# A two-layer diffusion block: buffers and queue order of the first layer's modulation, and the shape of three later modulation units

## The chip, the cores and the metric

The kernel runs on one core of one Trainium2 chip. The metric is the device time of one execution in microseconds (us); lower is better. One more execution was recorded by the hardware profiler; its own time stands beside the others below.

## The reference, cut to what matters

Two layers work on 512 latent tokens and 256 context tokens of width 1024. At the head of each layer a vector `c` (for the latents) and a vector `c_ctx` (for the context) give six modulation vectors through one matrix product each; the first two of them shift and scale the normalised tokens before the input projection.

```python
mod = (c_act @ w_mod[l] + b_mod[l])[:, None, :]
sh1, sc1, g1, sh2, sc2, g2 = jnp.split(mod, 6, axis=-1)
modc = cc_act @ w_mod[l] + b_mod[l]          # the same for the context
h  = rms_norm(x,  g_mix[l]) * (1 + sc1)  + sh1
hc = rms_norm(xc, g_mix[l]) * (1 + csc1) + csh1
aq, ak, av, bu, bv, cin, dq, dk, dv = split_cols(h @ w_in[l])
# four head groups (attention, gating, pooling, attention), then
x = x + g1 * (mix @ w_out[l])
x = x + g2 * swiglu(rms_norm(x, g_ffn[l]) * (1 + sc2) + sh2, ...)
```

## The kernel before

Data is feature-major: 8 tiles `x[k]` of 128 features by 768 tokens. Weights are split into a high and a low part (`wsplit`, L75: ScalarE copies at L82, VectorE subtracts at L83), and a product of two split operands is three matmuls (`mm3`, L63, lines L65 to L67). The kernel is written as a program without an order between engines; a planner with a simulated clock makes the order of each engine's queue from it when the kernel is built, and each queue then runs strictly in that order. `issue_after(x)` tells the planner that what stands in its block comes behind `x` in the queue of `x`'s engine. Tiles of one tag share a fixed number of buffers (`BUFS`), PSUM banks likewise (`BANKS`).

**The start of layer 0.** The string `START` (L27) gives the order in which steps are written down: `s` is a modulation slab (`mod_slab`, L193), `x` a load of a token tile with its squares, `w` the load and split of half of the first three weight units. Slab k holds the shift and the scale for feature tile k: it is 1 MB of weights, loaded as two halves of 512 KB into the tag `h` (8 buffers). Its 8 matmuls (L200) have 32 output partitions and 256 columns each, four of them side by side in PSUM bank `md`; ScalarE copies the result into a tile `rows` of tag `mraw` (L203), TensorE transposes it into bank `tq` (L143), and three small VectorE operations (L206 to L208) make shift and scale. Then `scaled` (L248, at L253 and L254) makes `hu[k]`, the scaled and split token tile. Slabs 4 to 7 take the `h` buffers that slabs 0 to 3 leave.

The norm runs beside it. `norm_scale` (L287) sums the squares on TensorE (L292, bank `tq`) and takes the inverse root on VectorE; `norm_spread` (L296) spreads it over the partitions (L302) and ScalarE evicts it (L304). They are written behind slab 4 and slab 5, and both spreads use bank `md`, so in that bank they stand ahead of slabs 6 and 7.

Then for k = 0 to 7 the three first units multiply `hu[k]` (`scaled_proj`, L260, from L441: a round of 18 matmuls), and a fourth unit, `win_dv` 1, does the same over all k in banks `tq` and `md` with its weights in tag `mraw` (L443 to L445). `normalise` (L448) makes the normalised tiles `h[k]` on VectorE, ScalarE and GpSimd (L312 to L317), for k from 2 on behind `hu[7]` in the queues. `d_proj(0)` is the first to multiply them (`tok_proj`, L550), from bank `pj`, which `c_take` (L795, at L799) has to empty first.

**Later units.** `mod_unit` (L146) is called three times in layer 0 (L893, L898, L902) for the units 4, 2 and 3. For each of four pairs of 512 KB pieces in tag `mraw` (2 buffers) it issues four matmuls of 32 output partitions and 512 columns, two for each piece (L154); rows are copied (L157), transposed in four steps and added up by four VectorE operations (L138). The planner fits these matmuls between those of the head groups.

Of the kernel before, what the change touches and what calls it, by code (L numbers as in the profile page):

```python
# [11 lines left out]
AF = mybir.ActivationFunctionType  # L12
OP = mybir.AluOpType
# [4 lines left out]
KT = 8  # L18
# [6 lines left out]
ORDER = (4, 6, 5, 7, 0, 2, 3, 1)  # L25

START = "s0 x1 x0 s1 w0 x2 x3 s2 x4 x5 s3 x6 x7 w1 s4 s5 s6 s7"  # L27
EPS = 1e-6
BIG = 1e30
W = 24 + NT  # L30
# [9 lines left out]
def hybrid_block(ctx: ExitStack, tc, t, out):  # L40
    nc = tc.nc
    V, S, G, T = nc.vector, nc.scalar, nc.gpsimd, nc.tensor
# [7 lines left out]
    def tile(tag, shape, dtype=F32):  # L50
        return sb.tile(shape, dtype, tag=tag, name=tag, bufs=BUFS[tag])

    def psum(tag):
        return psp.tile([128, 512], F32, tag=tag, name=tag, bufs=BANKS[tag])
# [14 lines left out]
    def load_raw(src, tag, size=1024):  # L69
        n = src.free_size()  # L70
        raw = tile(tag, [128, size])
        nc.sync.dma_start(raw[:, :n], src)
        return raw[:, :n]
# [43 lines left out]
        return x  # L117

    cc = const_tile("cc", [128, KT, 2], t["cc"])
    slabs = {k: [load_raw(t["wslab"][k, i], "h") for i in range(2)] for k in range(1)}  # L120
    ident = const_tile("ident", [128, 128], t["ident"])
    ones = const_tile("ones", [128, 32])
    V.memset(ones, 1.0)
    cact = const_tile("cact", [128, KT, 32])
# [7 lines left out]
    def mod_out(mods, pt, groups):  # L132

        m, bm = mods["m"], mods["bm"]
        for u, n, v, cols in groups:
            for i, c in enumerate(cols):
                b = bm[:, u, n].unsqueeze(2).to_broadcast([128, 4, v]) if i == 0 else m[:, u, n, :, 0:v]
                V.tensor_tensor(m[:, u, n, :, 0:v], pt[:, :, c], b, op=OP.add)  # L138

    def transposed(rows, n, tag="md"):  # L140
        pt = psum(tag).rearrange("p (s q) -> p s q", q=128)
        for s in range(n):
            T.transpose(pt[:, s, :], rows[:, 128 * s:128 * s + 128], ident)  # L143
        return pt

    def mod_unit(u, mods, tag="mraw"):  # L146

        ps = psum("md")
        for kk in range(4):
            raws = [load_raw(t["wmod"][mods["l"], u, 2 * kk + i], tag) for i in range(2)]  # L150
            for i in range(2):
                for n in range(2):
                    j = 2 * i + n
                    T.matmul(ps[32 * j:32 * j + 32, :], cact[:, 2 * kk + i, :],  # L154
                             raws[i][:, 512 * n:512 * n + 512], start=kk == 0, stop=kk == 3)
        rows = tile("mraw", [128, 512])
        S.activation(rows, ps, AF.Copy)  # L157
        pt = transposed(rows, 4)
        mod_out(mods, pt, [(u, n, 2, (slice(32 * n, 32 * n + 2), slice(64 + 32 * n, 66 + 32 * n))) for n in range(2)])

    def mod_vector(units, mods, v):

# [30 lines left out]
    def mod_slab(k, mods, bg):  # L193

        m, bm, l = mods["m"], mods["bm"], mods["l"]
        ps = psum("md")
        for i in range(2):
            raw = slabs[k][i] if k in slabs else load_raw(t["wslab"][k, i], "h")
            for j in range(4):
                T.matmul(ps[32 * j:32 * j + 32, :256], cact[:, 4 * i + j, :], raw[:, 256 * j:256 * j + 256],  # L200
                         start=i == 0, stop=i == 1)
        rows = tile("mraw", [128, 512])
        S.activation(rows[:, :256], ps[:, :256], AF.Copy)  # L203
        pt = transposed(rows, 2, "tq")
        red = small.tile([128, 2, 2], F32, tag="red", name="red")
        V.tensor_reduce(red, pt[:, 0:2].rearrange("p s (j x) -> p s x j", x=32)[:, :, 0:2], axis=AX.X, op=OP.add)  # L206
        V.tensor_scalar(m[:, k // 4, 0, k % 4], red[:, 0], bm[:, k // 4, 0, k % 4:k % 4 + 1], None, op0=OP.add)
        V.tensor_scalar(mods["a"][:, 0, k], red[:, 1], mods["g"][:, 0, k:k + 1], bg[:, k:k + 1],  # L208
                        op0=OP.mult, op1=OP.add)

    def new_mod(l):
        return {"l": l, "m": const.tile([128, 6, 2, 4, 2], F32, name=f"mod{l}"),
# [17 lines left out]
    segs_all = ((0, SEQ, 0), (SEQ, NT, 1))  # L230
# [29 lines left out]
    def scaled_proj(w, h, cuts, pss, k):  # L260
        for (c0, c1, *_), ps in zip(cuts[0], pss):
            mm3(ps[:, :c1 - c0], wf(w, k, 0), wf(w, k, 1), h[:, 0, c0:c1], h[:, 1, c0:c1], k == 0, k == KT - 1)
# [22 lines left out]
    marks = {}  # L285

    def norm_scale(sq, segs):  # L287

        n = segs[-1][1] // 128
        ps = psum("tq")  # L290
        for i in range(n):
            marks["scale"] = T.matmul(ps[:, i:i + 1], sq.acc[:, 128 * i:128 * i + 128], ones[:, 0:1],  # L292
                                      start=True, stop=True)
        return rsqrt(ps[:, :n], n, 1.0 / D, EPS)

# [78 lines left out]
    mods = [new_mod(0)]  # L374
# [11 lines left out]
    for l in range(DEPTH):  # L386
# [13 lines left out]
        if l == 0:  # L400
            xs, hu, ready = [None] * KT, [None] * KT, set()
            sq = Squares(segs_all)
            ws = [[], [], []]
            for what, k in START.split():
                k = int(k)
                if what == "w":
                    for w, (name, g) in zip(ws, first):
                        w += wsplit(t[name][0, g][:, 512 * k:512 * k + 512])
                    continue
                if what == "s":  # L410
                    mod_slab(k, mods[0], bg)
                else:
                    xs[k] = load_x(t["xt"][:, k])
                    sq.add(xs[k], G if k in (1, 3, 4, 5, 6, 7) else V)
                if k in ready:
                    hu[k] = scaled(xs[k], a[:, 0, k], shift(k), segs_all)
                ready.add(k)
                if what + str(k) == "s4":
                    rr = norm_scale(sq, segs_all)
                if what + str(k) == "s5":  # L420
                    r = norm_spread(rr, segs_all, ("md", "md"))
            first = ws
            mods.append(new_mod(1))
        else:
            r = norm_spread(norm_scale(sq, segs_all), segs_all, ("tq", "md"))
            first = [feat_units(*x) for x in first]
        fcuts = [cuts_lat if last else cuts_all] * 2 + [cuts_all]
        pss = [[psum(x) for x in y] for y in (("pj", "pj"), ("sc", "sc"), ("po", "pt"))]
        if last:

            for j, (w, ct, ps) in enumerate(zip(first, fcuts, pss)):
                for k in range(KT):
                    with ExitStack() as st:
                        for mark, n in (("scale", 6), ("spread", 10)):
                            if 8 * j + k >= n:
                                st.enter_context(tc.issue_after(marks[mark].ins))
                        scaled_proj(w, hu[k], ct, ps, k)
        else:
            for k in range(KT):
                for w, ct, ps in zip(first, fcuts, pss):  # L440
                    scaled_proj(w, hu[k], ct, ps, k)  # L441
        pss.append([psum(x) for x in ("tq", "md")])
        w = feat_units("win_dv", 1, "mraw")  # L443
        for k in range(KT):
# [485 lines left out]
        h = []  # L930
# [184 lines left out]
```

## Time and profile before

| | us |
|---|---|
| median of three runs | 1545.6 |
| lowest and highest | 1543.95, 1546.96 |
| the profiled execution | 1543.86 |
| its span, first to last instruction | 1542.1 |
| TensorE busy in the span | 1508.3 |
| VectorE busy | 956.9 |
| ScalarE busy | 618.8 |

The span is what the profiler's records cover; the execution's own time is 1.8 us longer. Where a time of an instruction is named below, it counts from the start of the span. Engines: PE is TensorE, PEld its weight loads, DVE VectorE, ACT ScalarE, POOL GpSimd, SP the engine whose queue issues the loads.

### The profile page before, as it was taken

What the parts mean: (1) busy time and instruction counts of PE and PEld (TensorE: products, weight loads), DVE (VectorE), ACT (ScalarE), POOL (GpSimd) and SP (SyncE); (2) the same over time, 40 slices, a digit from 0 to 9 for tenths busy, and PEclk for the clock granted to TensorE, in tenths of its full rate; (3) what the DMA queues carried; (4) which work ended last, traced back from release to release, by engine and by line L of the source; (5) the groups of instructions that cost most, each with busy time, mean ns of one, the idle gap of its engine ahead of it and who ended that gap; (6) DMA issues with size and microseconds to landing.
All of it is one profiled execution on the core that took longest, in us unless ns stands there. A gap on an engine that the chain in (4) does not pass through costs nothing.

```text
span 1542.1 us, 26166 instructions
## 1 busy us (share of the span) xinstructions
PE 1508.3 (98%) x10098; PEld 1330.2 (86%) x10098; DVE 956.9 (62%) x2317; ACT 618.8 (40%) x1278; POOL 118.3 (8%) x107
## 2 busy tenths in 40 slices
PE   6899999999999999999999999899999999999999
PEld 4788787788888888888888888889889998998997
DVE  3789877686485624843375458899865443544453
ACT  5547655643322112221222344477654332332331
POOL 2521200100000000000000004542000000000000
PEclk9999999999999999999999999999999999999999
DMA  8443223342243313722273232201232233233223
GB/s 313 128 144 102 93 80 108 126 141 76 89 144 111 122 62 101 234 62 63 82 230 96 71 105 76 83 32 44 89 101 90 93 94 98 90 88 105 89 86 100
DMA packets 79324, 163.39 MB, mean 106 GB/s; under 512 B 12000, under 2 KB 17760, under 8 KB 79200
## 3 DMA queue, kind: packets, MB, share of 16 engines
q1 hardware_dynamic: 79200, 161.73, 32.8%
q8 instruction: 79, 1.29, 0.3%
q14 instruction: 45, 0.37, 0.1%
HBM read 157.50 MB, written 4.19 MB: 105 GB/s over the span
## 4 chain that ended last, share of the span: by engine, by line
PE 87%; DVE 6%; DMA 4%; ACT 2%; issue 1%; POOL 1%; SPq 0%; ACTq 0%; POOLq 0%
PE pj L65 9%; PE pj L66 9%; PE pj L67 9%; PE sc L66 6%; PE sc L65 6%; PE sc L67 6%; PE tq L65 3%; PE tq L66 3%; PE tq L67 3%; PE po L66 3%; PE po L65 3%; PE po L67 3%; PE po L350 2%; PE pt L66 2%; PE pt L65 2%; PE pt L67 2%
## 5 line engine op out<-in xcount | busy, mean ns | idle before, releaser
L82 ACT ACTIVATE w<-raw 128x512 fp32r<-128x512 f32 x368 | 227.1, 621 | 617.6 <-PE sc L67 154.2
L83 DVE TENSOR_TENSOR w<-raw,w 128x512 fp32r<-128x512 f32 x336 | 226.7, 677 | 242.9 <-ACT w L82 242.6
L65 PE MATMUL pj<-w,h 128*128 128x256 f32 x480 | 138.4, 289 | 6.7 <-DVE post L499 5.9
L66 PE MATMUL pj<-w,h 128*128 128x256 f32 x480 | 138.7, 289 | 0.0
L67 PE MATMUL pj<-w,h 128*128 128x256 f32 x480 | 137.7, 287 | 0.0
L65 PE MATMUL pj<-st,w 128*128 128x258 f32 (+2 forms) x384 | 120.4, 314 | 2.5 <-ACT st L253 2.3
L66 PE MATMUL pj<-st,w 128*128 128x258 f32 (+2 forms) x384 | 120.0, 313 | 0.0
L66 PE MATMUL sc<-st,w 128*128 128x258 f32 (+2 forms) x384 | 119.8, 312 | 0.0
L65 PE MATMUL sc<-st,w 128*128 128x258 f32 (+2 forms) x384 | 119.7, 312 | 0.0
L67 PE MATMUL pj<-st,w 128*128 128x258 f32 (+2 forms) x384 | 119.5, 312 | 0.0
L67 PE MATMUL sc<-st,w 128*128 128x258 f32 (+2 forms) x384 | 118.9, 310 | 0.0
L65 PEld LDWEIGHTS pj<-w,h 128*128 128x128 f32 x480 | 92.1, 192 | 13.9 <-ACT post L494 5.5
L83 POOL TENSOR_TENSOR w<-raw,w 128x512 fp32r<-128x512 f32 x32 | 43.0, 1354 | 739.0 <-DVE row L283 633.3
L66 PEld LDWEIGHTS pj<-w,h 128*128 128x128 f32 x480 | 92.4, 192 | 1.7 <-DVE post L499 0.8
L67 PEld LDWEIGHTS pj<-w,h 128*128 128x128 f32 x480 | 92.3, 192 | 0.3 <-issue 0.2
L65 PEld LDWEIGHTS pj<-st,w 128*128 128x128 f32 x384 | 73.1, 190 | 9.5 <-ACT st L253 3.5
L67 PEld LDWEIGHTS pj<-st,w 128*128 128x128 f32 x384 | 72.6, 189 | 5.5 <-issue 1.7
L65 PEld LDWEIGHTS sc<-st,w 128*128 128x128 f32 x384 | 73.2, 191 | 4.5
L66 PEld LDWEIGHTS pj<-st,w 128*128 128x128 f32 x384 | 72.7, 189 | 4.8 <-issue 0.4
L66 PEld LDWEIGHTS sc<-st,w 128*128 128x128 f32 x384 | 72.7, 189 | 4.2
L67 PEld LDWEIGHTS sc<-st,w 128*128 128x128 f32 x384 | 72.3, 189 | 4.0
L65 PE MATMUL po<-st,w 128*128 128x512 f32 (+1 forms) x192 | 66.2, 345 | 0.0
(308 smaller groups left out, 4117.9 us busy)
## 6 DMA issues: line engine op xcount, KB each, us to landing
mraw<-in_wmod SPq DMA_DIRECT2D x80, 512.0 KB, 3.9
raw<-in_wg SPq DMA_DIRECT2D x88, 256.0 KB, 2.5
raw<-in_wu SPq DMA_DIRECT2D x88, 256.0 KB, 2.6
raw<-in_wd SPq DMA_DIRECT2D x64, 256.0 KB, 2.7
h<-in_wslab SPq DMA_DIRECT2D x16, 512.0 KB, 8.1
raw<-in_wout SPq DMA_DIRECT2D x32, 256.0 KB, 2.6
x<-in_xt SPq DMA_DIRECT2D x16, 384.0 KB, 5.4
raw<-in_wd SPq DMA_DIRECT2D x32, 192.0 KB, 2.4
```

The lines of the kernel that those rows point to most:

```text
L65: T.matmul(ps, ah, bh, start=start, stop=False)
L66: T.matmul(ps, ah, bl, start=False, stop=False)
L67: T.matmul(ps, al, bh, start=False, stop=stop)
L82: S.activation(w[:, 0, :n], raw, AF.Copy)
L83: eng.tensor_sub(w[:, 1, :n], raw, w[:, 0, :n].bitcast(F32))
L350: T.matmul(o[64 * hh:64 * hh + 64, :128], vs[hh][lo:hi], pts[i, hh], start=i == 0, stop=i == n - 1)
```

## The change

Slabs 1 to 3 stay in tag `h`, slab 4 is loaded into the two buffers of `mraw`, and slabs 5, 6 and 7 are loaded as four pieces of 256 KB each into buffers of `pts`, `T`, `post` and `bias`, tags that the head groups use later. So no slab has to wait for the buffer of another one. `rows` moves from `mraw` (two buffers) to `br` (one buffer, used next by the load of `d_k_gain`). `norm_scale` and `norm_spread` are written behind slab 7; the spread for the context uses bank `tq`, the one for the latents `md`. The rounds of products for k = 3, 4 and 5 are put behind the last transpose of slab 5, 6 and 7 in TensorE's queue (k = 6 and 7 behind that of slab 7 too), the round for k = 7 also behind the last matmul of the spread. `mod_unit` takes one 512 KB piece at a time and makes four matmuls of 256 columns from it, side by side in four groups of partitions, over eight pieces; it then needs a copy of 256 columns, two transposes and one VectorE operation.

```diff
+SPARE = {5: ("pts", "pts", "pts", "T"), 6: ("post", "post", "post", "post"), 7: ("T", "T", "bias", "bias")}
     def mod_unit(u, mods, tag="mraw"):
         ps = psum("md")
-        for kk in range(4):
-            raws = [load_raw(t["wmod"][mods["l"], u, 2 * kk + i], tag) for i in range(2)]
-            for i in range(2):
-                for n in range(2):
-                    j = 2 * i + n
-                    T.matmul(ps[32 * j:32 * j + 32, :], cact[:, 2 * kk + i, :],
-                             raws[i][:, 512 * n:512 * n + 512], start=kk == 0, stop=kk == 3)
+        for k in range(KT):
+            raw = load_raw(t["wmod"][mods["l"], u, k], tag)
+            for j in range(4):
+                T.matmul(ps[32 * j:32 * j + 32, :256], cact[:, k, :], raw[:, 256 * j:256 * j + 256],
+                         start=k == 0, stop=k == KT - 1)
         rows = tile("mraw", [128, 512])
-        S.activation(rows, ps, AF.Copy)
-        pt = transposed(rows, 4)
-        mod_out(mods, pt, [(u, n, 2, (slice(32 * n, 32 * n + 2), slice(64 + 32 * n, 66 + 32 * n))) for n in range(2)])
+        S.activation(rows[:, :256], ps[:, :256], AF.Copy)
+        pt = transposed(rows, 2)
+        V.tensor_tensor(m[:, u].rearrange("p n (j s) v -> p (n j) s v", s=2), ...)
     def mod_slab(k, mods, bg):
-            raw = slabs[k][i] if k in slabs else load_raw(t["wslab"][k, i], "h")
+            raws = slabs[k][2 * i:2 * i + 2] if k in SPARE else [slabs[k][i][:, x:x + 512] for x in (0, 512)]
-        rows = tile("mraw", [128, 512])
+        rows = tile("br", [128, 256])
+    def slab_load(k):
+        if k in SPARE:
+            slabs[k] = [load_raw(t["wslab"][k, x // 2][:, 512 * (x % 2):512 * (x % 2) + 512], tag, 512)
+                        for x, tag in enumerate(SPARE[k])]
+        elif k:
+            slabs[k] = [load_raw(t["wslab"][k, i], "mraw" if k == 4 else "h") for i in range(2)]
                 if what == "s":
+                    slab_load(k)
                     mod_slab(k, mods[0], bg)
-                if what + str(k) == "s4":
-                    rr = norm_scale(sq, segs_all)
-                if what + str(k) == "s5":
-                    r = norm_spread(rr, segs_all, ("md", "md"))
+            rr = norm_scale(sq, segs_all)
+            r = norm_spread(rr, segs_all, ("md", "tq"))
             for k in range(KT):
-                for w, ct, ps in zip(first, fcuts, pss):
-                    scaled_proj(w, hu[k], ct, ps, k)
+                with ExitStack() as st:
+                    if k > 2:
+                        st.enter_context(tc.issue_after(slab_end[min(k + 2, KT - 1)].ins))
+                    if k > 6:
+                        st.enter_context(tc.issue_after(marks["spread"].ins))
+                    for w, ct, ps in zip(first, fcuts, pss):
+                        scaled_proj(w, hu[k], ct, ps, k)
```

## Rows read from the trace of the kernel before

**Rows 1.** The page, part 1: busy time, share of span, instructions, by engine.
```profile
PE 1508.3 (98%) x10098; PEld 1330.2 (86%) x10098; DVE 956.9 (62%) x2317; ACT 618.8 (40%) x1278; POOL 118.3 (8%) x107
```
**Rows 2.** Windows: stretch, length, busy us by engine (instructions), PE clock, DMA share, GB/s.
```profile
0.00:72.50 72.50, 55.94 (x360) 40.44 (x360) 41.41 (x97) 38.79 (x78) 29.46 (x25) 0.98 0.65 227
72.50:280.00 207.50, 203.41 (x1606) 169.75 (x1606) 168.44 (x552) 121.95 (x293) 25.93 (x25) 1.00 0.33 108
```
**Rows 3.** Timeline of SP's queue: start, duration, line, what is loaded.
```profile
24.78 0.33 SPq L72 DMA_DIRECT2D raw<-in_win_dv  x1
...
35.93 0.43 SPq L464 DMA_DIRECT2D b_v_gain<-in_b_v_gain  x1
...
42.68 0.64 SPq L72 DMA_DIRECT2D h<-in_wslab  x1
```
**Rows 4.** Time to landing of the loads issued at 24.78 and at 42.68.
```profile
DMA to landing us min/median/max: 8.8/8.8/8.8
...
DMA to landing us min/median/max: 7.2/7.2/7.2
```
**Rows 5.** Windows inside the start, columns as in the second group.
```profile
4.00:32.00 28.00, 20.76 (x134) 12.76 (x134) 11.63 (x28) 14.71 (x29) 9.16 (x5) 1.00 1.02 388
...
47.80:55.60 7.80, 3.47 (x39) 1.56 (x39) 6.14 (x11) 6.34 (x14) 5.51 (x6) 1.00 0.34 124
55.60:58.60 3.00, 3.00 (x9) 2.52 (x10) 3.00 (x8) 2.23 (x6) 0.97 (x1) 0.50 0.64 208
```
**Rows 6.** Timeline of PE: start, duration, line, tiles, shapes, count [idle before, releaser].
```profile
26.38 0.51 PE L65 MATMUL pj<-st,w 128*128 128x512 f32 x1 [0.47 <-ACT st L253]
...
29.98 0.64 PE L200 MATMUL md<-h,cact 128*32 128x256 f32 x8
...
36.78 1.07 PE L200 MATMUL md<-h,cact 128*32 128x256 f32 x16
37.78 1.50 PE L292 MATMUL tq<-ones,row 128*128 128x1 f32 x12
...
49.43 1.07 PE L200 MATMUL md<-h,cact 128*32 128x256 f32 x16 [1.64 <-ACT row L304]
...
72.52 0.39 PE L65 MATMUL pj<-w,h 128*128 128x256 f32 x1 [0.56 <-DVE x L799]
```
**Rows 7.** Timeline of ACT: the second eviction of the spread norm.
```profile
48.80 0.57 ACT L304 ACTIVATE row<-md 128x512 f32<-128x512 f32 x1
```
**Rows 8.** Groups by line, DVE, 47.8 to 82.6 us: count, busy us, mean ns.
```profile
L317 DVE SCALAR_TENSOR_TENSOR h<-x,mod,h 128x256 fp32r<-128x256 f32 x8 | 6.5, 847 | 2.3 <-ACT h L316 2.3
L317 DVE SCALAR_TENSOR_TENSOR h<-x,mod,h 128x512 fp32r<-128x512 f32 x8 | 6.5, 818 | 0.0
L83 DVE TENSOR_TENSOR w<-raw,w 128x512 fp32r<-128x512 f32 x6 | 4.3, 744 | 0.0
L315 DVE SCALAR_TENSOR_TENSOR x<-x,a,row 128x512 f32<-128x512 f32 x4 | 2.7, 739 | 0.0
L315 DVE SCALAR_TENSOR_TENSOR x<-x,a,row 128x256 f32<-128x256 f32 x4 | 2.1, 558 | 0.0
```
**Rows 9.** Groups by line, PE, 72 to 300 us: the three later units and their transposes.
```profile
L154 PE MATMUL md<-mraw,cact 128*32 128x512 f32 x96 | 23.2, 604 | 2.1 <-DMA mraw<-in_wmod 1.1 <-issue 1.1
L143 PE MATMUL md<-ident,mraw 128*128 128x128 f32 x12 | 1.9, 277 | 0.0
```
**Rows 10.** Timeline of PE: groups of narrow matmuls, and what starts behind two of them.
```profile
20.44 0.64 PE L200 MATMUL md<-h,cact 128*32 128x256 f32 x8
21.01 0.50 PE L66 MATMUL pj<-st,w 128*128 128x512 f32 x1
...
155.65 1.04 PE L154 MATMUL md<-mraw,cact 128*32 128x512 f32 x2
156.62 0.55 PE L350 MATMUL po<-pts,row 128*64 128x128 f32 x6
...
252.86 1.07 PE L154 MATMUL md<-mraw,cact 128*32 128x512 f32 x8
```

More of the change, by code (lines that the diff above doesn't have):

```diff
@@ L119, in hybrid_block @@
     cc = const_tile("cc", [128, KT, 2], t["cc"])
-    slabs = {k: [load_raw(t["wslab"][k, i], "h") for i in range(2)] for k in range(1)}
+    slabs = {0: [load_raw(t["wslab"][0, i], "h") for i in range(2)]}
     ident = const_tile("ident", [128, 128], t["ident"])
@@ L138, in mod_out, with transposed @@
                 V.tensor_tensor(m[:, u, n, :, 0:v], pt[:, :, c], b, op=OP.add)
-    def transposed(rows, n, tag="md"):
+    slab_end = {}
+    def transposed(rows, n, tag="md", k=None):
         pt = psum(tag).rearrange("p (s q) -> p s q", q=128)
         for s in range(n):
-            T.transpose(pt[:, s, :], rows[:, 128 * s:128 * s + 128], ident)
+            slab_end[k] = T.transpose(pt[:, s, :], rows[:, 128 * s:128 * s + 128], ident)
         return pt
     def mod_unit(u, mods, tag="mraw"):
+        m, bm = mods["m"], mods["bm"]
         ps = psum("md")
-        for kk in range(4):
-            raws = [load_raw(t["wmod"][mods["l"], u, 2 * kk + i], tag) for i in range(2)]
-            for i in range(2):
-                for n in range(2):
-                    j = 2 * i + n
-                    T.matmul(ps[32 * j:32 * j + 32, :], cact[:, 2 * kk + i, :],
-                             raws[i][:, 512 * n:512 * n + 512], start=kk == 0, stop=kk == 3)
-        rows = tile("mraw", [128, 512])
-        S.activation(rows, ps, AF.Copy)
-        pt = transposed(rows, 4)
-        mod_out(mods, pt, [(u, n, 2, (slice(32 * n, 32 * n + 2), slice(64 + 32 * n, 66 + 32 * n))) for n in range(2)])
+        for k in range(KT):
[3 more added lines that the diff above has]
+                         start=k == 0, stop=k == KT - 1)
+        rows = tile("mraw", [128, 512])
+        S.activation(rows[:, :256], ps[:, :256], AF.Copy)
+        pt = transposed(rows, 2)
+        V.tensor_tensor(m[:, u].rearrange("p n (j s) v -> p (n j) s v", s=2),
+                        pt[:, 0:2].rearrange("p s (j x) -> p j s x", x=32)[:, :, :, 0:2],
+                        bm[:, u].rearrange("p n (j s) -> p (n j) s", s=2).unsqueeze(3).to_broadcast([128, 4, 2, 2]),
+                        op=OP.add)
     def mod_vector(units, mods, v):
@@ L197, in mod_slab @@
         for i in range(2):
-            raw = slabs[k][i] if k in slabs else load_raw(t["wslab"][k, i], "h")
+            raws = slabs[k][2 * i:2 * i + 2] if k in SPARE else [slabs[k][i][:, x:x + 512] for x in (0, 512)]
             for j in range(4):
-                T.matmul(ps[32 * j:32 * j + 32, :256], cact[:, 4 * i + j, :], raw[:, 256 * j:256 * j + 256],
-                         start=i == 0, stop=i == 1)
-        rows = tile("mraw", [128, 512])
-        S.activation(rows[:, :256], ps[:, :256], AF.Copy)
-        pt = transposed(rows, 2, "tq")
+                T.matmul(ps[32 * j:32 * j + 32, :256], cact[:, 4 * i + j, :],
+                         raws[j // 2][:, 256 * (j % 2):256 * (j % 2) + 256], start=i == 0, stop=i == 1)
+        rows = tile("br", [128, 256])
+        S.activation(rows, ps[:, :256], AF.Copy)
+        pt = transposed(rows, 2, "tq", k)
         red = small.tile([128, 2, 2], F32, tag="red", name="red")
```

## The prediction, made before the changed kernel was run

> **What bounds the kernel now.** I read the page's busy times first: TensorE is busy 1508.3 us, 98% of the span, and VectorE 62% [rows 1]. So what counts is a TensorE stretch that is idle, or work taken off TensorE. The windows by stage say where either can be found [rows 2]: of the first 72.5 us TensorE is busy for 55.9, so 16.6 us are idle there; from 72.5 to 280 us it is busy for 203.4 of 207.5, so there only less TensorE work helps, and VectorE with 168.4 of 207.5 us is not far behind. The change touches these two stretches and nothing later.
>
> Inside the start the reader should see two things. Up to 32 us the loads are the limit: they move 388 GB/s with the DMA engines full [rows 5]. From 47.8 to 55.6 us TensorE works for 3.5 of 7.8 us [rows 5], and neither loads nor arithmetic explain that: slab 6 waits 1.64 us for ScalarE to empty bank `md` of the spread norm [rows 6, 7], and slab 7 stands behind slab 6. Slab 7's last half was issued only at 42.68 us, behind small loads such as the broadcast gain at 35.93, and landed 7.2 us later, at 49.9 [rows 3, 4]. After the idle stretch the granted clock is 0.50 for 3 us, the 1.2 GHz level [rows 5]. The first product of `d_proj` comes at 72.52 us, 0.56 us after its bank was wanted [rows 6].
>
> **Change, part 1: own buffers, and the order in the start.** Slabs 6 and 7 no longer wait for `h` buffers, so their loads can stand right behind slab 5 and the second weights. The last of those weights was issued at 24.78 and landed 8.8 us later, at 33.6 [rows 3, 4]; slab 5 was issued before it. Behind it come 2.1 MB of slabs 6 and 7: at 388 GB/s [rows 5] 5.4 us, so slab 7 lands at about 39 instead of 49.9 us.
>
> TensorE then goes so: the round for k = 3 is held behind slab 5's transposes, at about 34 us (slab 5 there by 33.6, then the second half of its matmuls, a copy, two transposes). From there it has to do, until `d_proj`: five rounds of products of 3.5 us each (26.38 to 29.98 holds one round and a pair of transposes) [rows 6], 17.5; slabs 6 and 7 at 1.0 us each (36.78 to 37.78) [rows 6] and 0.3 for two transposes (12 take 1.9 us) [rows 9], 2.6; the column sums 1.5 [rows 6] and the spread, as many narrow matmuls, taken as the same, 3.0; `win_dv` 1, six matmuls for each k where a round has eighteen, a third of 8 x 3.5, 9.3. The sum is 32.4, so 66.4 us, and with 0.6 us for the gaps at the slabs 67 instead of 72.5: **5.5 us gained**. The half clock after 55.6 us goes with the idle stretch and is in this sum.
>
> What could take its place: `normalise`. The norm stands behind slab 7 now. Slab 7's transposes are done at about 41; before, the second spread was evicted at 49.4, 10 us behind the end of the column sums at 39.3 [rows 6, 7]. With 8 to 10 us again r is there at 49 to 52, no earlier than before. From there VectorE needs 6.5 + 6.5 + 2.7 + 2.1 us for the normalised tiles and 4 x 0.74 for the weight splits of `d_proj(0)` [rows 8], 20.8 us, so it ends at 70 to 73, while TensorE starts the context tiles at 67 and needs the last latent tile later. I take no cost for this; the other end is 3.5 us lost to the latent tiles. That is also why I don't count all of the 16.6 idle us.
>
> New waits, each with its queue. The rounds for k = 3 to 7 stand behind transposes in TensorE's queue, which runs in order: a late slab holds them and everything behind them; that is the second rival. `rows` has one buffer, so ScalarE's copy of the next slab waits for two transposes, 0.3 us [rows 9], beside loads that arrive 2.7 us apart (1 MB at 388 GB/s) [rows 5]: nothing, at most 0.3 us a slab. The load of `d_k_gain` waits in SP's queue for slab 7's transposes, with the `bias` and `win_d` loads behind it, from 35 to 41 us or later; the work that hides it is the rest of the start, 26 us of TensorE; without this cover it would cost its 6 us. The memset for `wpool` and the first `bias` tiles wait for slabs 6 and 7, long before they are needed: nothing.
>
> Between the ends (3.5 us lost to the latent tiles; 3.5 us more if `d_proj` profits from VectorE's earlier work too) part 1 gives 2 to 9 us, and I take 5.5, the value that the rows add up to.
>
> **Piece size, a rule against the change.** Half a slab in one load flowed at 388 GB/s beside 256 KB weight pieces [rows 5], so I price pieces at the same rate. The Trainium skill, page "DMA: Bandwidth & Descriptors", section "Rules for kernel authors", asks for at least 1 MiB in one DMA for the most bandwidth, and its fit gives a fixed 2.0 us with each; an estimate from that, if eight pieces of 256 KB went one behind the other at 2.6 us, puts slab 7's landing at 54 us. The windows speak against it, since many loads are in flight at once.
>
> **Change, part 2: three units in pieces.** A narrow matmul uses 32 of the 128 output partitions, and four of them run side by side if they stand together: one alone holds TensorE for 0.97 us (155.65 to 156.62), and a group of four has a record of 1.07 against its 1.04 [rows 10]. Before, two matmuls come with each piece, and the planner cut most groups in two: 24 pieces make some 22 groups of about a microsecond, 23.2 us in sum [rows 9], 21.7 without the overlap with what follows (1.04 - 0.97 for each). After it, a piece brings four matmuls of 256 columns, which have the form of half a slab: 0.57 us (20.44 to 21.01) [rows 10]. 24 x 0.57 = 13.7 us, so 8.0 us of TensorE go. Half of the twelve transposes go too, 1.9 us in all [rows 9]: at most 0.9, I take 0.5. VectorE and ScalarE lose a little work. **8.5 us of TensorE work** is the upper end. Not all of it need reach the end: TensorE is idle for only 4.1 us here, VectorE is busy for 81% [rows 2], and these matmuls now fill time in which a softmax runs on other engines. With that cover gone some waits show. I bound it at a half, 4 us, and at all, 8.5, and take three quarters, **6.3 us**, since TensorE is the fuller engine by 35 us. Two waits of 1.1 us for pieces [rows 9] can stay or go; they are inside these bounds.
>
> **Sum.** The profiled execution took 1543.86 us, its span 1542.1. 1543.9 - 5.5 - 6.3 = 1532.1. The median is 1.7 us above that execution, so **1533.8 us**. With both parts at their low and high ends: 1528 to 1540.
>
> **Rivals.**
> First, the start gives nothing: r is no earlier and VectorE's 20.8 us of normalising [rows 8] are the new limit. For it: r waits for slab 7 now. Against it: `hu[7]`, behind which most of `normalise` stands, is ready some 10 us earlier. Part 2 alone: 1539.3.
>
> Second, slower: slab 7 lands late and holds the last three rounds and the norm. Its place is TensorE's queue between 41 and 55 us. Each microsecond of landing behind 39 costs one; the 5.5 are used up at 44.5, the 6.3 of part 2 at 51, and from 54 us on the kernel is slower by more than 0.2%. For it: SP's issues run behind one another, and in the kernel before the same slab landed at 49.9 [rows 3, 4]; a stalled TensorE fell to the half clock [rows 5]. Against it: the pieces have buffers of their own, and the 388 GB/s. At 55 us: 1549. By the rule of the Trainium skill above it would be this case.
>
> Third, the change doesn't do what it says: the planner cuts each piece's four matmuls in two, as it cut the groups before. Then 48 x 0.57 = 27.4 us instead of 21.7 [rows 9, 10], 5.7 lost against 5.5 gained: 1545.8. Against it: all four now wait for one load, and slabs ran as whole groups [rows 6].
>
> Fourth, all of it arrives: 9 and 8.5 us, 1528.
>
> **How the numbers follow.** Forecast 0.62, start gives nothing 0.17, late slab 0.07, cut groups 0.07, all of it 0.07. A measurement of this kernel can tell about 0.2%, 3 us, from no change. Forecast, fourth and most of the first are faster by more than that: 0.83. The cut groups and a little of the first are the same: 0.09. Slower: 0.08, the late slab and a planner's order that comes out worse. The range takes in the bounds of both parts, 3 us for the order that the planner makes anew, and the first rival: 1525 to 1543; it leaves out the second and the third.
>
> **What would show it.** Right: slab 7 lands near 39 us; no gap above 2 us and no half clock between 40 and 60; the first `pj<-w,h` product of `d_proj` near 67; the later units 24 groups of 8 records, some 14 us in sum. Wrong: that product as late as before, with VectorE never idle behind r (first rival); TensorE waiting for slab 6 or 7 (second); groups of 4 records or fewer (third); TensorE gaps from 80 to 280 us grown by more than 4 us (the units' gain not passed on).

## The result and the profile after

The changed kernel takes **1556.1 us** (median; 1553.2 to 1557.5) beside 1545.0 us for the kernel before on the same chip, a ratio of **1.0067, 95% interval 1.0052 to 1.0081**: slower by about two thirds of a per cent, where 1533.8 us was forecast and 1543 was the upper end of the range. The profiled execution took 1557.5 us, its span is 1555.7, so there are 13.6 us to explain (1555.7 - 1542.1).

First the page, part 1, and the windows of [rows 2] again (stretch, length, busy us and instructions for PE, PEld, DVE, ACT and POOL, then PE clock, DMA share, GB/s).

```profile
PE 1514.9 (97%) x10188; PEld 1338.5 (86%) x10188; DVE 960.2 (62%) x2308; ACT 619.8 (40%) x1278; POOL 113.9 (7%) x107
```
```profile
0.00:72.50 72.50, 55.36 (x337) 38.92 (x338) 39.68 (x88) 39.02 (x79) 22.30 (x23) 0.91 0.64 227
72.50:280.00 207.50, 197.98 (x1615) 170.82 (x1613) 165.61 (x518) 115.31 (x273) 26.43 (x26) 0.97 0.30 96
```

TensorE was to be busy for less and is busy for 6.6 us more. The clock says why: 0.91 and 0.97 in the two stretches that had 0.98 and 1.00 [rows 2]. Where that time lies is seen in narrower windows of TensorE alone (stretch, length, busy, clock, DMA share, GB/s):

```profile
30.00:35.50 5.50, 3.33 (x20) 0.74 1.05 391
35.50:39.50 4.00, 4.00 (x14) 0.51 0.67 209
...
60.00:65.00 5.00, 4.17 (x16) 0.50 0.16 42
65.00:70.00 5.00, 5.00 (x26) 0.83 0.03 11
...
80.00:85.00 5.00, 3.13 (x15) 0.54 0.48 157
85.00:90.00 5.00, 5.00 (x35) 0.78 0.00 0
125.00:140.00 15.00, 12.39 (x82) 0.77 0.64 209
```

Four times the clock falls to 0.50, the 1.2 GHz level (the longer windows hold stretches at both levels). Busy time multiplied by the missing share of the clock gives 2.8 (3.33 x 0.26 + 4.00 x 0.49), 2.9 (4.17 x 0.50 + 5.00 x 0.17), 2.5 and 2.8 us. Before there was one such stretch [rows 5].

What stands ahead of the later three falls, and the steps of the start between them, are in TensorE's timeline (start, duration, line, tiles, shapes, count, and in brackets the idle time before it with its releaser):

```profile
43.38 0.61 PE L205 MATMUL md<-bias,cact 128*32 128x256 f32 x8
...
49.15 0.44 PE L146 MATMUL tq<-ident,br 128*128 128x128 f32 x2 [1.79 <-ACT br L208]
...
53.66 1.40 PE L305 MATMUL tq<-ones,row 128*128 128x1 f32 x12
...
60.83 1.19 PE L315 MATMUL tq<-ident,ry 128*128 128x128 f32 x4 [3.53 <-DVE ry L110]
...
81.86 0.55 PE L66 MATMUL pj<-w,h 128*128 128x256 f32 x1 [5.09 <-DVE x L817]
...
126.61 0.39 PE L381 MATMUL sc<-st 128*128 128x256 f32 x1 [1.49 <-DVE st L559]
```

The first product of `d_proj` comes at 81.86 us instead of 72.52 [rows 6]. Slab 7's last matmuls start at 43.38, its transposes only at 49.15, the column sums at 53.66 and the spread at 60.83, after TensorE was idle for 3.53 us. The rest of the chain is on ScalarE, VectorE and GpSimd (same columns):

```profile
46.65 0.20 ACT L93 ACTIVATE st<-mod 128x2 fp32r<-128x2 f32 x1 [4.14 <-DVE mod L212]
...
48.20 0.63 ACT L83 ACTIVATE mraw<-raw 128x512 fp32r<-128x512 f32 x1 [0.23 <-DMA raw<-in_win_dv]
48.73 0.37 ACT L208 ACTIVATE br<-md 128x256 f32<-128x256 f32 x1
...
62.12 0.38 ACT L317 ACTIVATE row<-tq 128x256 f32<-128x256 f32 x1 [5.05 <-PE tq L315]
63.76 0.60 ACT L317 ACTIVATE row<-md 128x512 f32<-128x512 f32 x1 [1.26 <-PE md L315]
```
```profile
46.10 0.17 DVE L490 TENSOR_SCALAR a_sink<-a_sink 128x4 f32<-128x4 f32 x1 [4.56 <-DMA a_sink<-in_a_sink]
46.18 0.17 DVE L211 TENSOR_REDUCE red<-tq 128x4 f32<-128x16 f32 x1
...
52.74 0.17 DVE L211 TENSOR_REDUCE red<-tq 128x4 f32<-128x16 f32 x1
...
55.22 0.16 DVE L101 TENSOR_SCALAR rx<-tq 128x6 f32<-128x6 f32 x1
57.10 0.69 DVE L84 TENSOR_TENSOR w<-raw,w 128x512 fp32r<-128x512 f32 x1 [1.72 <-ACT w L83]
57.71 0.69 DVE L102 TENSOR_SCALAR ry<-rx 128x6 int32<-128x6 int32 x1
...
62.53 8.82 DVE L328 SCALAR_TENSOR_TENSOR x<-x,a,row 128x256 f32<-128x256 f32 x8 [1.85 <-ACT row L317]
...
81.04 1.01 DVE L817 TENSOR_TENSOR x<-pj,row 128x512 f32<-128x512 f32 x2
```
```profile
63.59 10.62 POOL L326 TENSOR_TENSOR x<-x,row 128x256 f32<-128x256 f32 x8
```

Read them from the top. VectorE's reduction of slab 6 stands behind the scaling of `a_sink`, whose load lands at 46.1; ScalarE's row copy of slab 7 (48.73) stands behind the scaling for slab 6, which waits 4.14 us for that reduction, and behind a weight copy that waits for its own load; the second step of the inverse root stands behind a weight split. `r` is evicted at 62.12 and 63.76, where it was 46.19 and 48.80 [rows 7 has the second]. From there all sixteen pieces of `normalise` are still to do (eight tiles, each in a context and a latent part), and `c_take` (L817, 81.04), which releases `d_proj`, stands in VectorE's queue between them. VectorE is busy without a gap (a window as the first ones above):

```profile
70.00:80.00 10.00, 6.78 (x40) 5.78 (x38) 10.00 (x17) 6.59 (x12) 5.68 (x5) 1.00 0.20 54
```

**An account used below.** Up to the end of the last eviction of attention outputs that all traces share (ScalarE, `x<-po`; 316.1 us in before, 329.1 in after; the distance at the end of the spans is 0.6 us more), the time was cut into windows of a microsecond. Length minus busy is idle time; busy times (1 - granted clock) is loss by clock; what is left is TensorE's work at the full clock. Each figure is a sum over some 300 windows, an estimate therefore. The kernels are those of the experiments below; `r` is the start of its first eviction. The last three columns give idle time and loss by clock together, for three stretches (us).

| kernel | median us | r, first part | idle | clock | work left | 28-60 | 60-90 | 120-145 |
|---|---|---|---|---|---|---|---|---|
| before | 1545.0 | 46.2 | 21.7 | 1.6 | 292.8 | 7.7 | 1.6 | 0.0 |
| after | 1556.1 | 62.1 | 28.7 | 11.7 | 288.7 | 9.9 | 11.5 | 5.8 |
| e1_units | 1545.0 | 46.3 | 24.6 | 3.2 | 288.5 | 8.1 | 1.6 | 0.0 |
| e2_start | 1558.8 | 61.4 | 31.7 | 6.3 | 291.7 | 10.1 | 10.6 | 0.6 |
| e3_gains | 1556.1 | 63.3 | 33.0 | 6.3 | 289.3 | 10.1 | 12.0 | 3.7 |
| e4_order | 1551.9 | 57.0 | 30.1 | 6.1 | 288.0 | 5.9 | 16.5 | 0.9 |
| e5_nohold | 1548.5 | 59.8 | 29.0 | 3.5 | 288.0 | 4.2 | 12.8 | 0.0 |
| **e6_norm** | **1539.8** | 43.8 | 18.6 | 4.8 | 287.2 | 12.2 | 0.0 | 0.9 |
| e7_norm46 | 1551.1 | 46.3 | 23.9 | 5.6 | 288.4 | 5.8 | 8.0 | 0.0 |
| e8_vector | 1550.2 | 60.2 | 26.9 | 5.0 | 289.0 | 8.6 | 10.3 | 0.0 |
| e9_norm_nohold | 1544.5 | 43.8 | 25.5 | 2.9 | 287.4 | 9.1 | 2.0 | 0.3 |
| e10_norm_old_units | 1545.6 | 41.9 | 21.2 | 4.5 | 292.2 | 12.3 | 2.0 | 0.0 |
| e11_nohold_vector | 1547.9 | 61.9 | 28.8 | 4.0 | 287.8 | 6.7 | 13.0 | 0.5 |
| e12_norm_vector | 1546.0 | 43.4 | 23.0 | 5.2 | 286.4 | 13.4 | 0.0 | 0.4 |

So the change took 4.1 us of work off TensorE, and added 7.0 us of idle time and 10.1 us of half clock: 13.0 of the 13.6 us. More than half of those 17.1 us, 9.9 (11.5 - 1.6), lie between 60 and 90 us, 5.8 between 120 and 145, 2.2 between 28 and 60.

Each trace is of one execution. Those of e1, e7 and e9 differ among themselves by 7 to 8 us, and the traced one isn't always the middle: in e6 (1538.7) and e7 (1546.5) it is the shortest, in after (1557.5) and e9 (1547.0) the longest. A difference of one or two us between two rows shows nothing.

### The profile page after: what moved, and what is told of

The parts are those of the page before. It is cut to its first block, busy times and chain, and to the rows that moved or that the text cites. A ratio compares the mean times of both kernels' runs of the same rounds, so it can differ in the third digit from the quotient of the medians.

```text
span 1555.7 us, 26337 instructions
## 1 busy us (share of the span) xinstructions
PE 1514.9 (97%) x10188; PEld 1338.5 (86%) x10188; DVE 960.2 (62%) x2308; ACT 619.8 (40%) x1278; POOL 113.9 (7%) x107
## 4 chain that ended last, share of the span: by engine, by line
PE 87%; DVE 6%; DMA 4%; ACT 1%; issue 1%; SPq 0%; POOL 0%; ACTq 0%; DVEq 0%
PE pj L66 9%; PE pj L67 9%; PE pj L68 9%; PE sc L67 6%; PE sc L66 6%; PE sc L68 6%; PE tq L66 3%; PE tq L67 3%; PE tq L68 3%; PE po L67 3%; PE po L66 3%; PE po L68 3%; PE po L363 3%; PE pt L67 2%; PE pt L66 2%; PE pt L68 2%
## 5 line engine op out<-in xcount | busy, mean ns | idle before, releaser
L66 PE MATMUL pj<-w,h 128*128 128x256 f32 x480 | 141.4, 295 | 11.7 <-DVE post L517 6.4
L67 PE MATMUL pj<-w,h 128*128 128x256 f32 x480 | 140.8, 294 | 0.0
L68 PE MATMUL pj<-w,h 128*128 128x256 f32 x480 | 140.2, 292 | 0.0
L66 PEld LDWEIGHTS pj<-w,h 128*128 128x128 f32 x480 | 94.5, 197 | 17.5 <-issue 9.6
L68 PEld LDWEIGHTS pj<-w,h 128*128 128x128 f32 x480 | 94.5, 197 | 1.1 <-issue 0.9
L67 PEld LDWEIGHTS pj<-w,h 128*128 128x128 f32 x480 | 94.8, 197 | 0.8 <-issue 0.7
```

Of the source, the lines that this page charges most:

```text
L66: T.matmul(ps, ah, bh, start=start, stop=False)
L67: T.matmul(ps, ah, bl, start=False, stop=False)
L68: T.matmul(ps, al, bh, start=False, stop=stop)
```

## Experiments

### Which half of the change costs: e1_units, e2_start

The kernel before with the new `mod_unit` alone, and the changed kernel with the old one. In e1:

```diff
-        for kk in range(4):
-            raws = [load_raw(t["wmod"][mods["l"], u, 2 * kk + i], tag) for i in range(2)]
+        for k in range(KT):
+            raw = load_raw(t["wmod"][mods["l"], u, k], tag)
...
```


> The kernel before with the new mod_unit alone. If the units are worth what the changed kernel's trace shows of them (narrow matmuls hold TensorE 17.4 us there instead of 21.8), it is faster than before by 4 to 7 us, 1538 to 1541. If the units' waits for their pieces and the half clock behind them belong to the new form (as from 125 to 140 us in the changed kernel), it is no faster: 1545 or more.

> The changed kernel with the old mod_unit. If the loss is made in the start (d_proj begins 9.4 us later there, with more half clock behind it), it is slower than before by 12 to 17 us, 1557 to 1562. If the new units made the loss after 82 us, it is slower by 9 at most, 1554 or less.

e1: 1545.0 us, ratio 1.0005 (0.9993 to 1.0017). e2: 1558.8 us, ratio 1.0084 (1.0069 to 1.0100). The loss comes with the edits of the start. The units alone gave nothing: the account shows their 4.3 us of work gone (288.5 beside 292.8), and 4.5 us of idle time and clock in its place. 1.6 us of that lie in the first 50 us, which the edit doesn't touch: the planner makes the whole order anew for any edit, and how much of such a difference is its order and how much the spread of the executions one trace can't tell.

### Is it VectorE's order: e3_gains, e4_order

e3 holds the scaling of the gains and of `a_sink` behind slab 7's last VectorE operation; e4 holds it, and the splits of `win_dv` 1, of the first `win_d` and of `wpool`, behind the inverse root.

```diff
         nsink = bc_tile("a_sink", 4)
-        V.tensor_scalar(nsink, nsink, -1.0, None, op0=OP.mult)
+        with ExitStack() as st:
+            if l == 0:
+                st.enter_context(tc.issue_after(marks["norm"].ins))
+            V.tensor_scalar(nsink, nsink, -1.0, None, op0=OP.mult)
...
-        w = feat_units("win_dv", 1, "mraw")
+        with ExitStack() as st:
+            if l == 0:
+                st.enter_context(tc.issue_after(made[7][0]))
+                st.enter_context(tc.issue_after(marks["norm"].ins))
+            w = feat_units("win_dv", 1, "mraw")
```


> The changed kernel with the scaling of the small gains (a_q_gain, d_q_gain, a_sink) put behind slab 7's last operation in VectorE's queue. Theory, VectorE's order: slab 6's chain then doesn't wait for the load of a_sink (landed 46.1), which frees some 3 us of it, but the weight splits ahead of the root stay: 2 to 4 us faster than the changed kernel, 1552 to 1554. Rival, the holds on TensorE: no difference, 1556.

> The changed kernel with the gains, the splits of win_dv 1 and of win_d 0 and the split of wph all put behind the norm's inverse root on VectorE (and behind the scaling of token tile 7 on ScalarE). Theory, VectorE's order: the spread comes near 50 us instead of 61 and d_proj near 70 instead of 82; 10 to 16 us faster than the changed kernel, 1540 to 1546. Rival, the norm behind slab 7 is late whatever stands in VectorE's queue, or the holds on TensorE cost it: 1552 or more.

e3: 1556.1 us, ratio 1.0069 (1.0052 to 1.0086), no different from the changed kernel. e4: 1551.9 us, ratio 1.0044 (1.0029 to 1.0059). The theory missed in both; the times are those of the rivals (1556, and 1552 or more, at its edge). In e3 the wait only moved: slab 7's row copy starts at 50.64, right behind a weight copy (ScalarE's timeline):

```profile
50.11 0.63 ACT L84 ACTIVATE mraw<-raw 128x512 fp32r<-128x512 f32 x1 [6.64 <-DMA raw<-in_win_dv]
```

In e4 `r` is 5 us earlier, at 57.0, and TensorE's work of the start is through at 69.4, near the forecast's 67; then it has nothing to do. TensorE in windows and in its timeline, e4:

```profile
60.00:69.40 9.40, 9.40 (x54) 1.00 0.05 16
69.40:84.00 14.60, 1.08 (x11) 0.59 0.33 108
```
```profile
82.93 0.66 PE L644 MATMUL tq<-ident,row 128*128 128x128 f32 x2 [13.52 <-DVE sh L280]
```

So it is not mainly the small operations ahead of `r`. Everything behind `r` on VectorE, in e4 the held splits too, is still to be done when TensorE runs out of products that need no norm.

### Is it the late norm: e6_norm, e7_norm46

e6 writes the two parts of the norm behind slabs 4 and 5 again, both spreads in bank `md`. Buffers, order of the loads, holds and units stay as changed.

```diff
+                if what + str(k) == "s4":
+                    rr = norm_scale(sq, segs_all)
+                if what + str(k) == "s5":
+                    r = norm_spread(rr, segs_all, ("md", "md"))
-            rr = norm_scale(sq, segs_all)
-            r = norm_spread(rr, segs_all, ("md", "tq"))
```


> The changed kernel with the norm back behind slabs 4 and 5 and both spreads in bank md, as before; own buffers, holds and units as changed. Theory, the late norm: r is there near 47 to 50 us again, and d_proj comes at 70 to 75 instead of 82: 1542 to 1548. Rival, the holds or the order of VectorE's queue cost it: 1552 or more.

e7 writes the spread behind slab 6 with the context in `tq`, and holds the gains and the weight splits behind slab 7's work (in e4 they stand behind the inverse root).

> The changed kernel with the column sums behind slab 4 and the spreads behind slab 6 (banks md and tq), and with the gains and the weight splits of the start behind slab 7's work on VectorE and ScalarE. Theory, the late norm: r near 45 us while slabs 6 and 7 keep their early loads, d_proj at 66 to 72: 1536 to 1544, faster than the kernel before. Rival, nothing is gained since VectorE and GpSimd side by side set the pace of normalise: 1545 to 1550.

e6: **1539.8 us, ratio 0.9966 (0.9953 to 0.9979)**: 16.3 us faster than the changed kernel by one edit, better than expected, and faster than the kernel before. e7: 1551.1 us (1546.5 to 1554.7), ratio 1.0038 (1.0024 to 1.0051), a miss.

The evictions of `r` and TensorE's windows in e6:

```profile
43.84 0.38 ACT L317 ACTIVATE row<-md 128x256 f32<-128x256 f32 x1 [2.61 <-PE md L315]
...
45.47 0.59 ACT L317 ACTIVATE row<-md 128x512 f32<-128x512 f32 x1
```
```profile
50.00:60.00 10.00, 10.00 (x59) 0.83 0.41 134
60.00:80.00 20.00, 20.00 (x131) 1.00 0.18 58
```

With `r` 18 us earlier TensorE isn't idle at all between 50 and 80 us: VectorE and GpSimd normalise while the rounds of products run. The price is that the spreads stand ahead of slabs 6 and 7 in `md` and slab 7's transposes come at 55.9; from 28 to 60 us 12.2 us are lost beside 9.9 in after. In the account this is the clearest line: between 60 and 90 us the kernels with the norm behind slabs 4 and 5 (before, e1, e6, e9, e10, e12) lose 0 to 2.0 us, those with the norm behind slab 7 (after, e2 to e5, e8, e11) 10.3 to 16.5, whatever else was changed. A part of e6's gain isn't the norm's: the 5.8 us that after loses between 120 and 145 us are 0.9 in e6, as they are nearly gone in e5 and e8, which keep the late norm.

e7 has `r` early too, at 46.3, and `d_proj` starts at 70.3, but then stands:

```profile
77.35 0.58 PE L68 MATMUL pj<-w,h 128*128 128x256 f32 x1 [4.40 <-DVE w L85]
```

The weight splits that were held behind slab 7 are now what is late. Its time is therefore no evidence against the early norm. This trace is of its shortest execution, 4.6 us below its median; what the others waited for isn't recorded.

### The holds: e5_nohold, e9_norm_nohold

The rounds for k = 3 to 7 without `issue_after`; e5 in the changed kernel, e9 in e6.

```diff
-                    if k > 2:
-                        st.enter_context(tc.issue_after(slab_end[min(k + 2, KT - 1)].ins))
-                    if k > 6:
-                        st.enter_context(tc.issue_after(marks["spread"].ins))
```


> The changed kernel without the holds on TensorE (no issue_after for the rounds k = 3 to 7); buffers, norm behind slab 7 and units as changed. Theory, the late norm: the column sums still stand behind slab 7 in bank tq and normalise still waits for the spread, so 1551 to 1558. Rival, the holds are what costs: 1544 to 1549.

> The norm of the first layer is back behind slabs 4 and 5 (spreads in md), and the rounds of products for k = 3 to 7 are held behind no transposes; buffers, load order and units as in the changed kernel. Theory that the holds cost by themselves: with the early norm TensorE was still idle for 3.06 us before slab 6's group and 2.59 us before slab 7's transposes, and its clock was 0.70 in 30 to 40 us and 0.83 in 50 to 60; without holds the rounds fill these gaps, 4 to 6 us, so 1534 to 1536 us. Rival, that the holds cost only because they came on top of a late norm: 1538.5 to 1541 us, as with the early norm alone (1539.8).

e5: 1548.5 us, ratio 1.0021 (1.0012 to 1.0031), 7.6 us faster than the changed kernel; the rival was right. By the account that gain is clock, not idle time (29.0 beside 28.7 us idle, 3.5 beside 11.7 lost by clock), and it lies where the rounds run (4.2 beside 9.9 us lost between 28 and 60) and between 120 and 145 us (0 beside 5.8); the stretch behind the late norm gains nothing (12.8 beside 11.5). TensorE in e5:

```profile
30.00:40.00 10.00, 8.96 (x70) 1.00 0.87 304
60.00:70.00 10.00, 9.04 (x54) 1.00 0.25 78
70.00:80.00 10.00, 0.37 (x2) 0.67 0.26 92
80.00:85.00 5.00, 4.65 (x31) 0.64 0.32 105
125.00:140.00 15.00, 15.00 (x126) 1.00 0.48 153
```

It waits as long as the changed kernel, but nearly in one piece, 10.59 us ahead of 79.63, and has one fall behind that (an earlier one, 0.70 from 24 to 28 us, has no part in this).

e9: 1544.5 us, ratio 0.9992 (0.9984 to 1.0001), 4.7 us slower than e6. With an early norm the holds are worth something. The account of e9 has 6.9 us more idle time than e6 and 1.9 less lost by clock; part of it is a wait of 3.62 us for the row copy of a slab. These traces are of e9's longest execution and e6's shortest, 8.4 us apart. So neither theory on the holds was right: their sign depends on what else is late. Whether the holds as such or the planner's other choices make that difference, these runs can't tell.

### VectorE and GpSimd side by side: e8_vector, e11_nohold_vector, e12_norm_vector

The first layer's `normalise` wholly on VectorE, in the changed kernel (e8), in e5 (e11) and in e6 (e12).

```diff
-... G if k in [[0, 1, 3, 6], [2, 4, 6]][l] else V, seg)
+... G if k in [[], [2, 4, 6]][l] else V, seg)
```


> The changed kernel with all of layer 0's normalise on VectorE (GpSimd does none of its products, ScalarE none of their scalings): the price of VectorE and GpSimd side by side. In the changed kernel eight L328 products take 8.8 us while GpSimd does eight others in 10.6. If the two slow each other, sixteen on VectorE alone take about 10 us, d_proj comes no later than at 82 us, and the time is 1551 to 1557; if they don't, VectorE is 5 us later and the time 1558 to 1562.

> The changed kernel with the late norm kept, no holds on the rounds and the whole normalising of the first layer on VectorE. Alone the two edits gave 7.6 and 5.9 us against the changed kernel (1556.1). If they mend different stretches (the rounds before the norm, and the tiles behind it), they add up: 1541 to 1544 us. If both only shorten the same wait for the normalised tiles: 1546 to 1549 us.

> The norm of the first layer back behind slabs 4 and 5 (as in the kernel that took 1539.8 us), and the whole normalising of the first layer on VectorE instead of eight of its sixteen pieces on GpSimd. Theory that the two engines slow each other wherever they run side by side: eight pieces more on VectorE at 0.68 us are 5.4 us, but VectorE's other instructions there come back to their own length (sixteen of 0.76 to 0.61, 2.4 us; the slab's last operation 3.0 to 1.4 us in sum, 1.6 us), so VectorE ends about 1.4 us later: 1539 to 1542 us. Rival, that the slowing matters only where r is late and both engines start at once, and here GpSimd's eight pieces are a real help: 1543 to 1548 us. Faster than 1538 would mean that GpSimd's share costs even with the early norm.

e8: 1550.2 us, ratio 1.0034 (1.0022 to 1.0045), 5.9 us faster than the changed kernel although VectorE got eight more instructions, and just below the 1551 to 1557 of the theory. Groups by line and form, 40 to 90 us (count, busy us, mean ns), first after, on VectorE and on GpSimd, then e8:

```profile
L328 DVE SCALAR_TENSOR_TENSOR x<-x,a,row 128x512 f32<-128x512 f32 x4 | 5.8, 1501 | 0.0
...
L328 DVE SCALAR_TENSOR_TENSOR x<-x,a,row 128x256 f32<-128x256 f32 x4 | 3.1, 838 | 1.9 <-ACT row L317 1.9
```
```profile
L326 POOL TENSOR_TENSOR x<-x,row 128x512 f32<-128x512 f32 x4 | 6.8, 1746 | 0.0
```
```profile
L328 DVE SCALAR_TENSOR_TENSOR x<-x,a,row 128x512 f32<-128x512 f32 x8 | 5.5, 743 | 0.0
L328 DVE SCALAR_TENSOR_TENSOR x<-x,a,row 128x256 f32<-128x256 f32 x8 | 4.4, 623 | 1.3 <-ACT row L317 1.3
```

The same instruction takes 743 ns in e8, where GpSimd has no share in it, and 1501 ns in after beside GpSimd. In after, VectorE was busy for 8.8 us with its eight pieces and GpSimd for 10.6 with the other eight, side by side; in e8 VectorE did all sixteen in 9.9 (5.5 + 4.4). The helper made these products slower. The Trainium skill, page "SBUF — State Buffer", section "Who interferes with whom", says that VectorE and GpSimd have one pair of memory ports in common and that an instruction holds it as an exclusive lock; the doubled time agrees with that.

That this is what made e8 faster isn't shown. Its `d_proj` starts at 82.01, no earlier than in after (81.86), and 10.3 us are lost between 60 and 90 beside 11.5. Of the 8.2 us between the two traces at the end of the account (329.1 and 320.9), 5.8 lie at 120 to 145 us, where e8 loses none, far behind the normalising (TensorE in e8, as the windows of after):

```profile
125.00:140.00 15.00, 15.00 (x122) 1.00 0.43 140
```

e12: 1546.0 us, ratio 1.0005 (0.9996 to 1.0014), 6.2 us **slower** than e6, where the same edit had gained 5.9. The rival's range held. With the early norm the two engines do these products at different times (e6: GpSimd at 44.30, 46.14, 58.72 and 68.92, VectorE from 60.78 to 65.1), so GpSimd's share can be real help; e12 has 4.4 us more idle time than e6. The same instruction keeps its length in e6 even beside GpSimd's `bias` instruction, which takes the wait there (3256 ns, in e8 806 ns):

```profile
L328 DVE SCALAR_TENSOR_TENSOR x<-x,a,row 128x512 f32<-128x512 f32 x4 | 2.7, 748 | 0.0
```
```profile
L647 POOL TENSOR_TENSOR bias<-dmask,br 128x256 f32<-128x256 f32 x2 | 6.5, 3256 | 2.5 <-DMA br<-in_rpb 2.5
```

e11: 1547.9 us, ratio 1.0016 (1.0007 to 1.0024). The 7.6 us of e5 and the 5.9 of e8 don't add up; together they give 8.2. By the account the reason isn't the late stretch behind `r`, as its expectation had it (13.0 us lost there, 12.8 in e5, 10.3 in e8): both edits take away the same 5.8 us between 120 and 145, and that can be gained once.

### The units behind a start without the loss: e10_norm_old_units

e6 with the old `mod_unit`.

> The norm of the first layer back behind slabs 4 and 5, own buffers and holds as in the changed kernel, but the three later units with two loads and two matmuls of 512 columns each, as in the kernel before. If the units pass nothing on (as they did alone in the kernel before): 1538.5 to 1541 us, the same as with the new units (1539.8). If they pass their 4.4 us of TensorE work on here: 1543 to 1545 us.

e10: 1545.6 us, ratio 0.9998 (0.9989 to 1.0007), at the upper edge of what was expected if the units pass their work on. Two things follow. The new buffers, loads and holds with the early norm show no gain by themselves: slab 7's bytes are there some 11 us earlier, and the time is that of the kernel before. And the units in pieces, worth nothing in e1 and 2.7 us beside the late norm (e2 less after), are worth 5.8 us here. The account agrees: 292.2 us of work with the old units, 287.2 with the new, and idle and clock together 25.7 and 23.4.

## Why the prediction was wrong

**The failed step: when `r` is there.** The prediction put slab 7's transposes at 41 us and `r` 8 to 10 us later, at 49 to 52, "no earlier than before". They came at 49.15, and `r` 13 us behind them, at 62.12. Three terms were left out. Slab 7's matmuls (43.38) stand behind slab 6's and behind the round for k = 3, which the holds release at 36 us and which ran at a clock of 0.51. Its row copy waited on ScalarE behind slab 6's scaling, late by the load of `a_sink`, and a weight copy with a late load: it starts at 48.73, 4.7 us behind the end of slab 7's matmuls, where the prediction had put its wait at no more than 0.3 us. And the steps from there to `r` stand in VectorE's queue between weight splits that wait for loads. The 10 us between sums and spread in [rows 6, 7] were carried over as a length, though they held the same kind of waits.

**VectorE's 20.8 us behind `r` were taken to cost nothing.** `r` at 62.12 plus 20.8 is 82.9, and `d_proj` started at 81.86; that the two are so near is in part luck, since `d_proj` doesn't wait for the last tile, and the last tile came at 87.3, 25 us behind `r`. The sum had left out `c_take` and the other work in the same queue, and had no cost for the two engines side by side: L328 took 8.9 us (5.8 + 3.1), where [rows 8] have 4.8 from a stretch in which these products of the two engines don't overlap. So the first rival named the mechanism behind the larger part of the loss, but with `r` no later than before it came out at 1539.3. With `r` at 62.1 the same working would have put `d_proj` 10.4 us later than before, and with the units' 6.3 us the median at some 1550 us. In e4 (`r` at 57.0) the last tile came 25 us behind `r` too, and `d_proj` at 85.3, since `c_take` stood behind all of it. Whether `c_take` further ahead in VectorE's queue would mend part of it, no run tried.

**TensorE's sum of 32.4 us was about right, and didn't matter.** In e4 TensorE was through at 69.4, with 3.1 us lost by clock in the first 50 us of it. The forecast's 67 was the time at which TensorE could start `d_proj`, not the time at which its operands were there.

**Half clock.** "No half clock between 40 and 60" came true by the letter ("no gap above 2 us" didn't: the 3.53 us end at 60.83), and the loss sits beside it: 10.1 us more than before over the first 329 us, the largest single term. The prediction counted it as gone with the idle stretch and didn't ask which new waits would bring it back.

**Landing: right.** SP's timeline and time to landing in after:

```profile
32.47 1.00 SPq L73 DMA_DIRECT2D bias<-in_wslab  x2
...
DMA to landing us min/median/max: 5.3/5.4/5.4
```

The last piece of slab 7 was issued at 33.1 and landed at 38.5; 39 was forecast. From 30 to 35.5 us the loads moved 391 GB/s, slab pieces of 256 KB among them. The late-slab rival is out. The landing at 54 us that the prediction estimated from the fit on the Trainium skill's page "DMA: Bandwidth & Descriptors" (section "Anatomy of one DMA — SWDGE (gpsimd) path", where it stands for loads that GpSimd prepares; here SP issues them) didn't come; with many loads in flight no such price of a small piece shows. e10 adds that the earlier landing was no gain in time. `d_k_gain` was issued at 50.9 us, later than thought, and VectorE's instruction that reads it (53.94) had no idle time ahead of it (in e6 it waited 2.43 us for that load).

**Units: right in kind, too large in size.** TensorE's groups of the units in after, 72 to 315 us:

```profile
L156 PE MATMUL md<-mraw,cact 128*32 128x256 f32 x192 | 19.0, 400 | 0.7 <-DMA mraw<-in_wmod 0.6
L146 PE MATMUL md<-ident,mraw 128*128 128x128 f32 x6 | 1.2, 274 | 0.0
```

19.0 us in 26 groups are 17.2 without the overlap with what follows (0.07 us a group), where 13.7 was forecast against 21.7. Each matmul leaves two records here (192 for 96). Some groups of four were split into 2 and 6 records with 0.62 and 0.63 us, where 8 records take 0.64, and one ran at the lower clock (1.08 us for 8 records), so the third rival held in part. With the transposes the work saved is 4.1 to 5.6 us, not 8.5. How much of it arrives was guessed at three quarters; it was none in e1, and in e6 its 5.0 us (292.2 - 287.2) are there in full (5.8 us of median against e10). The sign at the end, "gaps from 80 to 280 us grown by more than 4 us", didn't come: they grew from 3.7 us in before to 6.4 in e1 and 6.3 in after.

**What stays open.** How much of a difference of 2 to 5 us belongs to an edit and how much to the planner's new order can't be told from these runs. Why TensorE stalls and slows between 120 and 145 us in after (5.8 us) and e3 (3.7), and in no other kernel by more than 0.9, isn't shown; it isn't the late norm alone, since e4, e5, e8 and e11 have that too. Why the holds help with the early norm is not settled.

## What to carry to other kernels

A step that many instructions on a second engine wait for (here the norm, with 20 us of normalising behind it) is better written as early as its inputs allow, even where it delays something that looks like the chain; price its move by the work queued behind it, not by its own length. An earlier load is worth only what somebody waits for it. And work taken off the fullest engine need not arrive at the end while other stalls can take it: try such an edit again when they are gone. Where a saving and a loss meet, sum idle time and lost clock by stretch before naming a cause: e8's gain lay mostly 50 us behind the instructions that it changed.

## What the runs showed of the hardware

VectorE's product with the row on 128x512 values (L328) takes 743 ns in e8 and 1501 ns in after, beside GpSimd's product with the same row; the GpSimd product took 1746 ns there against 1326 in before, so sixteen pieces split over both at once took longer (10.6 us) than all of them on VectorE (9.9). Which of the two is slowed isn't fixed: beside GpSimd's `bias` instruction in e6 the VectorE product kept 748 ns and GpSimd's instruction took 3256 ns in place of 806.

In after, waits of 3.53, 5.09 and 1.49 us on TensorE, 10.1 in sum, were each followed by a stretch at a granted clock of 0.50 to 0.83 that cost 2.5 to 2.9 us more, 8.2 together. In e5 one wait of 10.6 us (ahead of 80 us) was followed by one such stretch, 0.64 in 80 to 85 us, which cost 1.7 us (4.65 x 0.36). So in these two traces three short waits cost more than a long one of about their sum. Not every wait is followed by a fall: behind the 1.79 us ahead of 49.15 in after the clock stayed at 1.00 (windows of a microsecond from 49 to 54).
